# Both projections of the inputs ahead of both of the gates in the first mixer's units, and an input gate written in place

## The chip, the cores and the metric

The kernel runs on one core of a Trainium2 chip. The metric is the device time of one execution in microseconds; lower is better. The five engines of the core work side by side, each through its own row of instructions: TensorE (PE; its weight loads are listed apart as PEld), VectorE (DVE), ScalarE (ACT), GpSimd (POOL) and SyncE (SP), which starts the transfers.

## What is computed

One layer of a decoder: 2048 tokens of 1024 channels in f32. After a norm one projection feeds two mixers. The first is a gated linear recurrence over time behind a short convolution, with 512 channels in eight blocks; the second has four heads with a state of 128 x 128 each. Their outputs are joined, projected back and added; then a gate with a small embedding follows, and a last norm. The reference, cut to what matters:

```python
def rg_lru(x, wa, ba, wx, bx, lam):                     # first mixer
    xb = x.reshape(B, T, 8, 64)
    r = sigmoid(einsum('btgi,gij->btgj', xb, wa).reshape(B, T, 512) + ba)   # recurrence gate
    i = sigmoid(einsum('btgi,gij->btgj', xb, wx).reshape(B, T, 512) + bx)   # input gate
    log_a = -8.0 * r * softplus(-lam)
    a = exp(log_a)
    mult = sqrt(-expm1(2.0 * log_a))                    # 1 at the first token
    u = mult * (i * x)
    h[t] = a[t] * h[t - 1] + u[t]                       # written as an associative scan
    return h

def hgrn2_branch(q, fz, iv, g, lb, norm_w):             # second mixer
    f = lb + (1.0 - lb) * sigmoid(fz)
    k = (1.0 - lb) * sigmoid(-fz)
    o = gla_chunked(silu(q) * 128 ** -0.5, k, log(f), iv)   # scores, state per chunk, outputs
    return rms_norm_heads(o, norm_w) * silu(g)

u = rms_norm(x)
xa, ga, qb, fb, ib, gb = split(u @ w_in)
xa = causal_depthwise_conv(xa, conv_w, conv_b)          # width 4
ya = rg_lru(xa, ...) * silu(ga)
yb = hgrn2_branch(qb, fb, ib, gb, ...)
h = x + concat([ya, yb]) @ w_out
h = h + sigmoid(rms_norm(h) @ w_gate + b_gate) * (p @ w_ple)
return rms_norm(h)
```

## The kernel before

**Tiling.** The tokens are taken in two halves of 1024, each half as two blocks of 512 (b = 0, 1; `NB` is 512, `HT` 1024). Channels lie on the 128 partitions. Every large product is made of three matmuls, since each f32 operand is split into a high and a low part: high by high, high by low and low by high (`mm3`, L87 to 89). A projection of 1024 input channels into 128 output channels for one block is thus 24 matmuls of 128x128 by 512 columns (`project`).

**Units.** In each half a list, `orders`, gives the order of the units: in the first half v, v, a 0, fq 0, g 0, a 1, fq 1, a 2, fq 2, a 3, fq 3, g 1; in the second a 3 stands at the end, behind g 1. A unit has 256 columns of the input weights. They are loaded in four pieces (`load_w`): SyncE starts the transfer, ScalarE copies the high part (`whi`, L76), GpSimd subtracts for the low part (`wlo`, L77). There are two buffers for a unit's weights and two for raw pieces, so the pieces for a later unit follow when an earlier unit's last matmul frees its buffer.

**A unit a** (`unit_a`) is one of four pairs of channel blocks of the first mixer. For each block of tokens it projects the inputs xa; ScalarE brings them out of PSUM (L409), VectorE makes the convolution (L411, L414: one product, and three products with a sum), and the result is split (`xp`, L420 and 421). Then it projects the gate path ga (sigmoid L324 on ScalarE, product L325 on VectorE). The gates r and i are small matmuls on the split inputs, each followed by two sigmoids of 64 partitions (`gates`, L381): the matmul of c = 0 leaves r of the lower 64 channels in the lower partitions of its result and the input gate of the other 64 channels in the upper ones; c = 1 is the other way round. Here the input gate of every 64 channels goes into a tile `is_` in the partitions in which the result has it, and two copies on VectorE (L389) bring each part to its channels' partitions in `i_`. Behind block 1's gates stands the recurrence over all 1024 tokens (`recur`): the product of i and the inputs (L391), tanh, exponential, square and root on ScalarE (L392 to 396), two products (L395, L399), the scan (L400), the product with ga (L402) and the store of y.

**A unit fq** (`unit_b`, called for each of the two blocks) is one head of the second mixer: f and kn by sigmoids (L436, 437), f scaled (L438), a running product cp (scan, L443), its reciprocal rc (L445), factors per chunk (mid, rmid, dec), q (L465 to 467), kn (L460), then scores (L475, four matmuls of 128 columns from q and kn, masked into `sc_buf` at L477), a transposed kn (L481), the state's updates (L489 to 498, through `sp`, L497) and the outputs.

**Order.** Work that would wait is put off by a counter: `after(n, fn)` files a function and `tick()`, behind each projection, runs what is due. Gates are filed for three ticks later, scores for two. This gives the order in which the code hands out work; the order on each engine is then set by the framework's scheduler from its own estimates. Behind the units come the output projection, the gate and the last norm, in 16 tiles of 128 tokens; y goes through memory, and its split is L76 and L77 once more (`yh`, `yl`).

Of the kernel before, what the change touches and what calls it, by code (L numbers as in the profile page):

```python
# [8 lines left out]
F32 = mybir.dt.float32  # L9
# [10 lines left out]
P = 128  # L20
# [3 lines left out]
NB = 512  # L24
# [13 lines left out]
def hymba_block(ctx: ExitStack, tc: tile.TileContext, x, xT, pT, w_in, vecs, rg_w, w_out, w_gate,  # L38
# [191 lines left out]
    def tick():  # L230
        clock[0] += 1
        run_due()
# [82 lines left out]
    def half(hf):  # L315
        def project(w, half, b, name):
            acc = pj(name)
            cs = slice(half * P, (half + 1) * P)
            for k in range(KT):
                mm3(acc, w[0][:, k, cs], w[1][:, k, cs], u_hi[hf][b][:, k, :], u_lo[hf][b][:, k, :], k == 0, k == KT - 1)  # L320
            return acc

        def silu_into(dst, acc):
            nc.scalar.activation(dst, acc, AF.Sigmoid)  # L324
            nc.vector.tensor_tensor(dst, acc, dst, ALU.mult)  # L325
# [38 lines left out]
        def unit_a(w, j):  # L364
# [3 lines left out]
            ga = ap.tile([P, HT], F32, tag="ga", name=f"ga_{nm}")  # L368
            r = ap.tile([P, HT], F32, tag="r", name=f"r_{nm}")
            i_ = ap.tile([P, HT], F32, tag="i", name=f"i_{nm}")  # L370
            is_ = ap.tile([P, HT], F32, tag="th", name=f"is_{nm}")
            nc.vector.tensor_copy(xa[:, 0:3], halo[:, j, :])

            def gates(b, xp):
                s = slice(b * NB, (b + 1) * NB)
                for c in range(2):
                    pg = gl(f"rg_{nm}_{b}_{c}")
                    nc.tensor.matmul(pg, lhsT=g_hi[:, 2 * j + c, :], rhs=xp[c], start=True, stop=False)
                    nc.tensor.matmul(pg, lhsT=g_lo[:, 2 * j + c, :], rhs=xp[c], start=False, stop=True)
                    for dst, vb, h in ((r, V_BA, lohi[c]), (is_, V_BX, lohi[1 - c])):  # L380
                        nc.scalar.activation(dst[h, s], pg[h], AF.Sigmoid, bias=vec[h, vb + j:vb + j + 1])  # L381
                if b == 1:
                    recur()

            def recur():

                nc.vector.tensor_copy(halo[:, j, :], xa[:, HT:HT + 3])
                for c in range(2):
                    nc.vector.tensor_copy(i_[lohi[c]], is_[lohi[1 - c]])  # L389
                th = ap.tile([P, HT], F32, tag="th", name=f"th_{nm}")  # L390
                nc.vector.tensor_tensor(i_, i_, xc, ALU.mult)  # L391
                nc.scalar.activation(th, r, AF.Tanh, scale=sp8[:, j:j + 1])  # L392
# [13 lines left out]
            for b in range(2):  # L406
# [14 lines left out]
                    nc.vector.tensor_tensor(xp[c][o], xc[m, s], xp[c][m].bitcast(F32), ALU.subtract)  # L421
                after(3, lambda b=b, xp=xp: gates(b, xp))
                tick()
                acc = project(w, 1, b, f"ga_{nm}_{b}")
                silu_into(ga[:, s], acc)
                tick()

        def unit_b(w, j, b):
# [316 lines left out]
```

## Time and profile before

| | us |
|---|---|
| median of three runs | 1080.12 (1077.13 to 1081.25) |
| the profiled execution | 1079.53 |
| its span in the trace | 1077.3 |
| TensorE busy | 1035.1 (96%) |
| VectorE busy | 743.0 (69%) |
| ScalarE busy | 459.3 (43%) |
| GpSimd busy | 268.6 (25%) |

Busy times are sums over the span. The chain (part 4 of the profile) follows the work that ended last back from its end and gives the share of each engine in it. The mean granted clock of TensorE in this execution is 0.983 of full speed.

### The profile page before, as it was taken

The page shows a single profiled execution, that of the slowest core. Times are in us where ns is not written, and L with a number is a line of the kernel's source. Part 1 is how long each engine was busy: PE and PEld are TensorE (multiplying, and loading weights), DVE is VectorE, ACT ScalarE, POOL GpSimd, SP SyncE. Part 2 cuts the span into 40 slices and gives each one's busy share as a digit, 9 for nine tenths or more (in the row PEclk, how much of TensorE's full clock was granted, in tenths as well). Part 3 has the DMA queues.
Part 4 walks back from the last instruction along what each step waited for, and adds up shares of the span by engine and source line. Part 5 has one row for each costly group of instructions (what it writes and reads, how often), then busy time and mean ns, then how long its engine had stood idle before and what let it go on. Part 6 is the DMA issues. An engine that isn't in the chain of part 4 may idle for free.

```text
span 1077.3 us, 13808 instructions
## 1 busy us (share of the span) xinstructions
PE 1035.1 (96%) x5192; PEld 880.3 (82%) x5192; DVE 743.0 (69%) x1373; ACT 459.3 (43%) x779; POOL 268.6 (25%) x238
## 2 busy tenths in 40 slices
PE   8999999999999999999899999899999999999997
PEld 7998788787878998788787888677888888888886
DVE  6836746868688506745869839899766677666764
ACT  5546426556566225634656327642222222223222
POOL 5131221222223032221222217541112221111110
PEclk9999999999999999999999999899999999999998
DMA  9421111111136211111111038351122222111101
GB/s 332 138 78 42 59 59 40 59 59 59 59 128 233 70 59 59 59 59 40 59 59 53 26 123 273 112 162 64 64 84 83 74 69 74 64 64 59 44 25 54
DMA packets 55266, 91.10 MB, mean 85 GB/s; under 512 B 4640, under 2 KB 25120, under 8 KB 55200
## 3 DMA queue, kind: packets, MB, share of 16 engines
q1 hardware_dynamic: 55200, 90.22, 25.2%
q8 instruction: 41, 0.67, 0.2%
q14 instruction: 25, 0.20, 0.1%
HBM read 73.43 MB, written 16.78 MB: 84 GB/s over the span
## 4 chain that ended last, share of the span: by engine, by line
PE 76%; DVE 14%; DMA 4%; issue 2%; ACT 2%; POOL 1%; SPq 0%; POOLq 0%; DVEq 0%; ACTq 0%
PE g L88 7%; PE g L89 6%; PE g L87 6%; PE o L89 4%; PE o L87 4%; PE o L88 4%; PE q L88 3%; PE q L87 3%; PE v L89 2%; PE v L88 2%; DVE rc L445 2%; PE q L89 2%; PE v L87 2%; PE f L89 2%; PE f L88 2%; PE f L87 2%
## 5 line engine op out<-in xcount | busy, mean ns | idle before, releaser
L77 POOL TENSOR_TENSOR wlo<-raw_w,whi 128x512 fp32r<-128x512 f32 x92 | 126.2, 1384 | 300.0 <-ACT whi L76 299.6
L208 DVE STREAM_TRANSPOSE u2T<-u 32x256 f32<-32x256 f32 x256 | 111.6, 436 | 3.8
L89 PE MATMUL o<-wo_hi,yl 128*128 128x512 f32 x256 | 100.6, 394 | 3.5 <-POOL yl L77 3.5
L76 ACT ACTIVATE whi<-raw_w 128x512 fp32r<-128x512 f32 x96 | 58.0, 627 | 104.0 <-DMA raw_w<-in_w_in 81.9
L87 PE MATMUL o<-wo_hi,yh 128*128 128x512 f32 x256 | 100.7, 393 | 0.4 <-ACT yh L76 0.4
L88 PE MATMUL o<-wo_lo,yh 128*128 128x512 f32 x256 | 100.5, 392 | 0.0
L88 PE MATMUL g<-wg_lo,u2uh 128*128 128x512 f32 x224 | 88.0, 393 | 2.7 <-DVE wg_lo L77 2.7
L87 PE MATMUL g<-wg_hi,u2uh 128*128 128x512 f32 x224 | 88.1, 393 | 1.0 <-ACT wg_hi L76 1.0
L89 PE MATMUL g<-wg_hi,u2ul 128*128 128x512 f32 x224 | 87.6, 392 | 0.0
L89 PE MATMUL v<-whi,ul 128*128 128x256 f32 x224 | 64.7, 290 | 3.4 <-DVE ul L77 3.3
L88 PE MATMUL v<-wlo,uh 128*128 128x256 f32 x224 | 64.4, 288 | 0.8 <-POOL wlo L77 0.7
L87 PE MATMUL v<-whi,uh 128*128 128x256 f32 x224 | 64.3, 288 | 0.0
L77 POOL TENSOR_TENSOR yl<-raw_y,yh 128x512 fp32r<-128x512 f32 x32 | 43.2, 1354 | 78.1 <-ACT yh L76 64.4
L89 PEld LDWEIGHTS o<-wo_hi,yl 128*128 128x128 f32 x256 | 48.7, 190 | 14.2 <-POOL yl L77 4.0
L87 PEld LDWEIGHTS o<-wo_hi,yh 128*128 128x128 f32 x256 | 48.6, 190 | 11.0 <-ACT yh L76 0.9
L88 PEld LDWEIGHTS o<-wo_lo,yh 128*128 128x128 f32 x256 | 48.6, 190 | 10.1
L411 DVE TENSOR_SCALAR xc<-xa,vec 128x512 f32<-128x512 f32 x16 | 11.4, 712 | 65.6 <-ACT xa L409 65.6
L183 POOL TENSOR_TENSOR rs_f<-ms_f,neg_half 128x1 f32<-128x1 f32 x16 | 8.8, 549 | 189.9 <-DVE ms_f L181 175.9
L76 ACT ACTIVATE yh<-raw_y 128x512 fp32r<-128x512 f32 x32 | 19.9, 629 | 83.9 <-issue 47.5
L652 ACT ACTIVATE gt<-gt 128x512 f32<-128x512 f32 (+1 forms) x33 | 20.2, 613 | 82.0 <-DVE gt L651 81.9
L445 DVE RECIPROCAL rc<-cp 128x512 f32<-128x512 f32 x16 | 53.6, 3349 | 0.3
L497 ACT ACTIVATE sp<-state,dec 128x128 f32<-128x128 f32 x60 | 24.0, 401 | 69.6 <-DVE state L498 50.1
(221 smaller groups left out, 2915.2 us busy)
## 6 DMA issues: line engine op xcount, KB each, us to landing
raw_w<-in_w_in SPq DMA_DIRECT2D x96, 256.0 KB, 3.0
xcm<-in_xT SPq DMA_DIRECT2D x18, 512.0 KB, 4.3
xt<-in_x SPq DMA_DIRECT2D x16, 512.0 KB, 5.4
raw_y<-y_dram SPq DMA_DIRECT2D x32, 256.0 KB, 2.8
h<-in_x SPq DMA_DIRECT2D x16, 512.0 KB, 3.6
out<-h SPq DMA_DIRECT2D x15, 512.0 KB, 2.6
y_dram<-ga SPq DMA_DIRECT2D x16, 256.0 KB, 2.5
y_dram<-yb SPq DMA_DIRECT2D x16, 256.0 KB, 2.2
```

Source lines behind the costliest of these rows:

```text
L76: nc.scalar.activation(hi, src, AF.Identity)
L77: lo_eng.tensor_tensor(lo, src, hi.bitcast(F32), ALU.subtract)
L87: nc.tensor.matmul(acc, lhsT=lh, rhs=rh, start=first, stop=False)
L88: nc.tensor.matmul(acc, lhsT=lh, rhs=rl, start=False, stop=False)
L89: nc.tensor.matmul(acc, lhsT=ll, rhs=rh, start=False, stop=last)
L183: nc.gpsimd.tensor_tensor(rs, ms, neg_half[:, 0:1], ALU.pow)
L208: nc.vector.transpose(dst[32 * j:32 * j + 32, :, 32 * i:32 * i + 32], src[32 * i:32 * i + 32, :, 32 * j:32 * j + 32])
L411: nc.vector.tensor_scalar(xc[:, s], xa[:, b * NB:b * NB + NB], cw[:, 0:1], vec[:, V_CONVB + j:V_CONVB + j + 1], ALU.mult, ALU.add)
L445: nc.vector.reciprocal(rc, cp)
L497: nc.scalar.activation(sp, state[j], AF.Identity, scale=dec[:, n])
L652: nc.scalar.activation(gt, gt, AF.Sigmoid)
```

## The change

In `unit_a` the loop over the blocks becomes two loops: xa of block 0 and xa of block 1 first, each with its convolution and its filing of the gates, and then ga of block 0 and ga of block 1. The number of ticks is the same, so the gates of block 1, filed at the second tick instead of the third, come due one tick earlier: at the end of the unit instead of behind the next unit's first projection. The recurrence goes with them. And the tile `is_` goes: ScalarE writes the input gate straight into the partitions of its channels in `i_`, from the partitions of the matmul's result on the other side, and the two copies of 64 partitions by 1024 fall away.

```diff
--- before.py
+++ after.py
@@ -368,7 +368,6 @@
             ga = ap.tile([P, HT], F32, tag="ga", name=f"ga_{nm}")
             r = ap.tile([P, HT], F32, tag="r", name=f"r_{nm}")
             i_ = ap.tile([P, HT], F32, tag="i", name=f"i_{nm}")
-            is_ = ap.tile([P, HT], F32, tag="th", name=f"is_{nm}")
             nc.vector.tensor_copy(xa[:, 0:3], halo[:, j, :])
 
             def gates(b, xp):
@@ -377,16 +376,15 @@
                     pg = gl(f"rg_{nm}_{b}_{c}")
                     nc.tensor.matmul(pg, lhsT=g_hi[:, 2 * j + c, :], rhs=xp[c], start=True, stop=False)
                     nc.tensor.matmul(pg, lhsT=g_lo[:, 2 * j + c, :], rhs=xp[c], start=False, stop=True)
-                    for dst, vb, h in ((r, V_BA, lohi[c]), (is_, V_BX, lohi[1 - c])):
-                        nc.scalar.activation(dst[h, s], pg[h], AF.Sigmoid, bias=vec[h, vb + j:vb + j + 1])
+
+                    for dst, vb, h in ((r, V_BA, lohi[c]), (i_, V_BX, lohi[1 - c])):
+                        nc.scalar.activation(dst[lohi[c], s], pg[h], AF.Sigmoid, bias=vec[h, vb + j:vb + j + 1])
                 if b == 1:
                     recur()
 
             def recur():
 
                 nc.vector.tensor_copy(halo[:, j, :], xa[:, HT:HT + 3])
-                for c in range(2):
-                    nc.vector.tensor_copy(i_[lohi[c]], is_[lohi[1 - c]])
                 th = ap.tile([P, HT], F32, tag="th", name=f"th_{nm}")
                 nc.vector.tensor_tensor(i_, i_, xc, ALU.mult)
                 nc.scalar.activation(th, r, AF.Tanh, scale=sp8[:, j:j + 1])
@@ -421,8 +419,9 @@
                     nc.vector.tensor_tensor(xp[c][o], xc[m, s], xp[c][m].bitcast(F32), ALU.subtract)
                 after(3, lambda b=b, xp=xp: gates(b, xp))
                 tick()
+            for b in range(2):
                 acc = project(w, 1, b, f"ga_{nm}_{b}")
-                silu_into(ga[:, s], acc)
+                silu_into(ga[:, b * NB:(b + 1) * NB], acc)
                 tick()
 
         def unit_b(w, j, b):
```

VectorE in the first half, from the kn of unit fq 1's block 0 to the mask of its scores. A name ends in unit, block and a number; `th`, `i`, `r` and `ga` belong to the recurrence of unit a 1, which runs just ahead of fq 1. Before:

```order
L460 SCALAR_TENSOR_TENSOR kn_1_0_1681<-kn_1_0_1681,omlb,rc_1_0_1689 128x512
L395 SCALAR_TENSOR_TENSOR th_1_1714<-xc_1_1495,th_1_1714 128x1024
L438 TENSOR_SCALAR f_1_1_1782<-f_1_1_1782,omlb,lb 128x512
L440 COPY d_115<-f_1_1_1782 128x8
L441 MEMSET f_1_1_1782 128x8
L443 SCALAR_TENSOR_TENSOR cp_1_1_1789<-f_1_1_1782,d_115 128x512
L398 MEMSET th_1_1714 128x1
L399 TENSOR_TENSOR i_1_1498<-i_1_1498,th_1_1714 128x1024
L445 RECIPROCAL rc_1_1_1791<-cp_1_1_1789 128x512
L450 COPY mid_1_1_1793<-cp_1_1_1789 128x4
L400 SCALAR_TENSOR_TENSOR r_1_1497<-r_1_1497,h_last,i_1_1498 128x1024
L477 COPY_PREDICATED sc_buf_113<-keep,sc_1_0_1804 128x512
```

Now, from the recurrence's scan to the same unit's q of block 1:

```order
L398 SCALAR_TENSOR_TENSOR r_1_1494<-r_1_1494,h_last,i_1_1495 128x1024
L466 TENSOR_TENSOR q_1_0_1747<-q_1_0_1747,cp_1_0_1708 128x512
L459 SCALAR_TENSOR_TENSOR kn_1_0_1702<-kn_1_0_1702,omlb,rc_1_0_1710 128x512
L437 TENSOR_SCALAR f_1_1_1776<-f_1_1_1776,omlb,lb 128x512
L399 COPY h_last<-r_1_1494 128x1
L400 TENSOR_TENSOR ga_1_1493<-ga_1_1493,r_1_1494 128x1024
L439 COPY d_115<-f_1_1_1776 128x8
L440 MEMSET f_1_1_1776 128x8
L442 SCALAR_TENSOR_TENSOR cp_1_1_1783<-f_1_1_1776,d_115 128x512
L444 RECIPROCAL rc_1_1_1785<-cp_1_1_1783 128x512
L449 COPY mid_1_1_1787<-cp_1_1_1783 128x4
L465 SCALAR_TENSOR_TENSOR q_1_1_1836<-q_1_1_1811,q_1_1_1836 128x512
```

The recurrence's scan and its product with ga stood behind the reciprocal of block 1; now the scan stands ahead of the kn of block 0 and the product right behind f of block 1.

ScalarE in the same unit, from the first pieces of the next unit a's weights (`whi_8`) to q of block 0, before:

```order
L76 ACTIVATE whi_8_1861<-raw_w_8_0_1863 128x512
L76 ACTIVATE whi_8_1861<-raw_w_8_1_1867 128x512
L324 ACTIVATE ga_1_1496<-ga_1_1_1610 128x512
L76 ACTIVATE whi_8_1861<-raw_w_8_2_1871 128x512
L76 ACTIVATE whi_8_1861<-raw_w_8_3_1875 128x512
L436 ACTIVATE f_1_0_1680<-f_1_0_1655 128x512
L437 ACTIVATE kn_1_0_1681<-f_1_0_1655 128x512
L381 ACTIVATE r_1_1497<-rg_1_1_0_1701,vec 64x512
L381 ACTIVATE is_1_1499<-rg_1_1_0_1701,vec 64x512
L381 ACTIVATE r_1_1497<-rg_1_1_1_1706,vec 64x512
L381 ACTIVATE is_1_1499<-rg_1_1_1_1706,vec 64x512
L465 ACTIVATE q_1_0_1753<-q_1_0_1728 128x512
```

Now, from the gate path's last sigmoid to f:

```order
L324 ACTIVATE ga_1_1493<-ga_1_1_1606 128x512
L381 ACTIVATE r_1_1494<-rg_1_1_0_1633,vec 64x512
L381 ACTIVATE i_1_1495<-rg_1_1_0_1633,vec 64x512
L381 ACTIVATE r_1_1494<-rg_1_1_1_1638,vec 64x512
L381 ACTIVATE i_1_1495<-rg_1_1_1_1638,vec 64x512
L390 ACTIVATE th_1_1644<-r_1_1494,sp_127 128x1024
L76 ACTIVATE whi_8_1855<-raw_w_8_2_1865 128x512
L391 ACT_TABLE_LOAD
L391 ACTIVATE r_1_1494<-r_1_1494,nsp_128 128x1024
L76 ACTIVATE whi_8_1855<-raw_w_8_3_1869 128x512
L435 ACT_TABLE_LOAD
L435 ACTIVATE f_1_0_1701<-f_1_0_1676 128x512
```

f and kn of block 0 stood ahead of the gates of block 1; now the four gate sigmoids, the tanh, the exponential and two loads of function tables stand ahead of f.

TensorE at the scores of block 0 of the same unit, before, inside the projection of q of block 1:

```order
L88 MATMUL q_1_1_1817<-ul_1_389,whi_5_1637 128x512
L89 MATMUL q_1_1_1817<-uh_1_388,wlo_5_1638 128x512
L87 MATMUL q_1_1_1817<-uh_1_388,whi_5_1637 128x512
L475 MATMUL sc_1_0_1804<-q_1_0_1753,kn_1_0_1681 128x128 x4
L481 MATMUL kT_1_0_1810<-ident,kn_1_0_1681 128x128 x4
L88 MATMUL q_1_1_1817<-ul_1_389,whi_5_1637 128x512
L89 MATMUL q_1_1_1817<-uh_1_388,wlo_5_1638 128x512
L87 MATMUL q_1_1_1817<-uh_1_388,whi_5_1637 128x512
```

Now, inside the next unit's first projection:

```order
L87 MATMUL q_1_1_1811<-uh_1_388,whi_5_1658 128x512
L88 MATMUL q_1_1_1811<-ul_1_389,whi_5_1658 128x512
L89 MATMUL q_1_1_1811<-uh_1_388,wlo_5_1659 128x512
L87 MATMUL xa_2_0_1879<-uh_0_210,whi_8_1855 128x512
L88 MATMUL xa_2_0_1879<-ul_0_211,whi_8_1855 128x512
L89 MATMUL xa_2_0_1879<-uh_0_210,wlo_8_1856 128x512
L87 MATMUL xa_2_0_1879<-uh_0_210,whi_8_1855 128x512
L88 MATMUL xa_2_0_1879<-ul_0_211,whi_8_1855 128x512
L89 MATMUL xa_2_0_1879<-uh_0_210,wlo_8_1856 128x512
L474 MATMUL sc_1_0_1798<-q_1_0_1747,kn_1_0_1702 128x128 x4
L480 MATMUL kT_1_0_1804<-ident,kn_1_0_1702 128x128 x4
```

The scores moved eleven matmuls back, out of q and into xa of unit a 2. The scores of block 1 (`sc_1_1`) stand 70 matmuls of projections behind the end of f of block 1 in the order before, and 60 in the new one.

## Rows read from the trace of the kernel before

**Rows 1.** Page, parts 1 and 4: busy us; shares of the last chain

```profile
PE 1035.1 (96%) x5192; PEld 880.3 (82%) x5192; DVE 743.0 (69%) x1373; ACT 459.3 (43%) x779; POOL 268.6 (25%) x238
...
PE 76%; DVE 14%; DMA 4%; issue 2%; ACT 2%; POOL 1%; SPq 0%; POOLq 0%; DVEq 0%; ACTq 0%
```

**Rows 2.** List of waits: who for whom, total us, times, longest

```profile
PE sc L475 <- DVE kn L460: 16.1, 7, 3.0
...
PE o L89 <- POOL yl L77: 3.5, 1, 3.5
```

**Rows 3.** TensorE by time, 188 to 207: start, us, instruction [idle before]

```profile
189.84 1.05 PE L475 MATMUL sc<-q,kn 128*128 128x128 f32 x8
...
202.08 0.39 PE L87 MATMUL ga<-uh,whi 128*128 128x512 f32 x1
...
203.44 0.39 PE L87 MATMUL ga<-uh,whi 128*128 128x512 f32 x1
206.20 1.02 PE L475 MATMUL sc<-q,kn 128*128 128x128 f32 x7 [2.37 <-DVE kn L460]
```

**Rows 4.** ScalarE by time, 168 to 190

```profile
169.34 0.58 ACT L324 ACTIVATE ga<-ga 128x512 f32<-128x512 f32 x1
173.22 0.63 ACT L76 ACTIVATE whi<-raw_w 128x512 fp32r<-128x512 f32 x1 [3.31 <-DMA raw_w<-in_w_in]
...
174.80 0.58 ACT L436 ACTIVATE f<-f 128x512 f32<-128x512 f32 x1
...
175.75 0.67 ACT L381 ACTIVATE r<-rg,vec 64x512 f32<-64x512 f32 x1
...
177.71 0.68 ACT L381 ACTIVATE is<-rg,vec 64x512 f32<-64x512 f32 x1
...
183.31 1.15 ACT L392 ACTIVATE th<-r,sp 128x1024 f32<-128x1024 f32 x1 [2.42 <-DVE i L389]
184.48 1.28 ACT L393 ACT_TABLE_LOAD   x1
185.77 1.15 ACT L393 ACTIVATE r<-r,nsp 128x1024 f32<-128x1024 f32 x1
```

**Rows 5.** VectorE by time, 168 to 210

```profile
175.41 1.35 DVE L438 TENSOR_SCALAR f<-f,omlb,lb 128x512 f32<-128x512 f32 x1 [4.77 <-ACT f L436]
...
178.41 0.69 DVE L389 COPY i<-is 64x1024 f32<-64x1024 f32 x1
...
184.05 1.22 DVE L391 TENSOR_TENSOR i<-i,xc 128x1024 f32<-128x1024 f32 x1
...
188.05 1.23 DVE L395 SCALAR_TENSOR_TENSOR th<-xc,th 128x1024 f32<-128x1024 f32 x1 [0.84 <-ACT xc L394]
189.96 0.55 DVE L438 TENSOR_SCALAR f<-f,omlb,lb 128x512 f32<-128x512 f32 x1 [0.69 <-ACT f L436]
...
192.85 0.06 DVE L398 MEMSET th<- 128x1 f32 x1 [0.73 <-ACT th L396]
...
199.62 0.73 DVE L477 COPY_PREDICATED sc_buf<-keep,sc 128x512 f32<-128x512 uint32 x1
...
200.81 1.26 DVE L455 TENSOR_TENSOR dec<-cp,mid 128x3 f32<-128x3 f32 x1
...
205.31 0.74 DVE L460 SCALAR_TENSOR_TENSOR kn<-kn,omlb,rc 128x512 f32<-128x512 f32 x1
```

**Rows 6.** GpSimd by time, 168 to 202

```profile
173.94 2.55 POOL L77 TENSOR_TENSOR wlo<-raw_w,whi 128x512 fp32r<-128x512 f32 x2 [2.40 <-ACT whi L76]
193.87 2.70 POOL L77 TENSOR_TENSOR wlo<-raw_w,whi 128x512 fp32r<-128x512 f32 x2 [17.38 <-ACT whi L76]
198.97 3.08 POOL L77 TENSOR_TENSOR wlo<-raw_w,whi 128x512 fp32r<-128x512 f32 x2 [2.40 <-ACT whi L76]
```

**Rows 7.** VectorE by time, 412 to 455, one row

```profile
448.12 1.92 DVE L402 TENSOR_TENSOR ga<-ga,r 128x1024 f32<-128x1024 f32 x1
```

**Rows 8.** A stretch: us, busy PE PEld DVE ACT POOL, PEclk, DMA, GB/s

```profile
207.60:211.00 3.40, 3.40 (x18) 3.30 (x17) 2.67 (x6) 2.51 (x5) 0.00 (x0) 0.51 0.10 34
```

## The prediction

> **What bounds the kernel now.** I read the page first, then the list of who waited for whom, then one stretch in order of time, engine by engine. TensorE is busy 96% of the span and holds three quarters of the chain that ended last; the next holder is VectorE with 14% [rows 1]. So an edit can gain only where TensorE stands still, and the list of waits says where that is: 16.1 us in seven waits of one kind, the scores of a head of the second group (line 475) waiting for kn from VectorE (line 460) [rows 2]. The only other long wait that this change can touch is one of 3.5 us for yl at the start of the output projection [rows 2].
>
> The seven waits stand behind units of the first group: unit a hands its recurrence to VectorE and ScalarE just as the next unit fq needs both. I take one of them as the model, the scores of block 1 of fq 1 in the first half. TensorE's last matmul ahead of it starts at 203.44 and the scores at 206.20, of which 2.37 us is the wait [rows 3]; TensorE was ready at 203.83. From 202.08 to 203.44 are six matmuls of 512 columns [rows 3], so one costs 0.227 us.
>
> **What the change takes away.** Two copies of 0.69 us leave VectorE in each of the eight units a (the 178.41 row is one, [rows 5]): 1.4 us a unit, 11 us in all, but only what lies on the chain to kn counts. The product of the input gate and the input (184.05, 1.22 us, of which some 0.1 overlaps the next) now stands ahead of f, where VectorE is idle, so 1.1 us leave the chain too. VectorE also stood idle three times in the chain, 0.84, 0.69 and 0.73 us, each time for ScalarE [rows 5]; in the new order other work stands in each of these places. And f of block 0, held at 175.41 for 0.8 us beyond the 0.55 of its twin at 189.96, no longer meets GpSimd's work. From the start of f at 175.41 to the end of the last kn at 206.05 are 30.6 us [rows 5]; without these pieces, 30.6 - 1.4 - 1.1 - 2.3 - 0.8 = 25.0 us.
>
> **What it adds: f comes later.** In the kernel before, ScalarE evicts f right behind the weights' last piece, at 174.80 [rows 4]. Now both gates, the tanh, a table load, the exponential and a second table load stand ahead of it. By the rows: the gate path's sigmoid ends at 169.92; four gate sigmoids take 2.64 us (175.75 to 178.39); the tanh 1.15, which gives 173.7; a weight piece 0.63 (its data are there at 173.22); table load 1.28; exponential 1.15; weight piece 0.63; table load 1.28; f itself 0.58 [rows 4]. The sum is 179.2, against 175.4: f is 3.8 us later. Nothing covers that, since VectorE has nothing else to do between 174 and 179: the rest of the recurrence needs the exponential, which comes as late. The chain then ends at 179.2 + 25.0 = 204.2, 1.9 us earlier than the 206.05 of before.
>
> On the table load a rule speaks against the change: the Trainium skill, "ScalarE: Activation LUTs", section "What ACT_TABLE_LOAD costs", gives about 2.66 us for a switch, of which 1.38 us are a drain. The rows have 1.28 us for the load, the exponential 0.01 us behind it and the load 0.02 us behind the tanh [rows 4]: the trace shows no drain. By the Trainium skill's price the total below would be some 19 us longer, an estimate of 1106 us.
>
> **What it moves: TensorE's turn.** Counted from the end of f 1, before, 19 matmuls of q stood ahead of the scores of block 0, and 5 + 17 + 7 + 22 more ahead of those of block 1, 70 in all; now 30 and 30 do. TensorE reaches block 1's scores ten matmuls sooner, at 203.83 - 10 x 0.227 = 201.6. With kn at 204.2 and 0.15 us from its end to the first scores [rows 3, 5] the wait is 2.7 us, against 2.4. So what VectorE gains is given back by TensorE's arriving earlier: 0.3 us lost. Counted alike, five stretches have nine or ten matmuls fewer and two have six; those two gain 0.6 us each by the same sum.
>
> **What else stands in the new place.** GpSimd works in pairs of about 1.3 us on weight pieces. The pair at 193.87 fell beside VectorE's reciprocal and held nobody up; the pair at 173.94 fell on f, which took 1.35 us; the second piece of the pair at 198.97 fell on dec, which took 1.26 us for 3 columns [rows 5, 6]. In the new order the earlier of the two later pairs follows the last matmul of q 1, whose weights' buffer it fills: that matmul ends about 191.1 (189.84 and five matmuls, [rows 3]), ScalarE's copy of 0.63 follows, and GpSimd starts about 191.9. From f of block 1 to its kn are 16.1 us (189.96 to 206.05); from f of block 0 to its kn the new order has th where that stretch has ga, 1.2 us each, and lacks the idle 0.73, dec's hold of 1.1 and the masking of scores with the short operations beside it (199.62 to 200.81), some 1.3: 12.9 are left [rows 5]. So VectorE reaches f of block 1 at 179.2 + 12.9 = 192.1, and right behind it stands the product ga, which took 1.92 us where it met such a pair [rows 7], 0.7 more than the product of the same shape at 184.05. So between 0 and 0.8 + 0.7, with an op of a few columns between them that can lose 0.5 more, is added. Both pieces of the pair are still to run when f arrives, so I take a value nearer to the upper end, 1.1 us. The hold on dec stays as it was.
>
> Per stretch that is 0.3 + 1.1 = 1.4 us more on five, and 1.1 - 0.6 = 0.5 us more on two: 8.0 us. In the first stretch of each half the gate sigmoids of block 0 now queue behind two more splits, each of about the 0.63 us of a weight piece; half of that hidden, 0.6 us each. Together 9 us.
>
> **Edits with one answer.** The input gate's sigmoid, 0.68 us beside its twin's 0.67 [rows 4], now writes to the other 64 partitions; the twin is the nearest row, so I take it as nothing. Were it twice as long, f would come 1.4 us later per stretch; were it shorter, it could save at most as much. The store of y moves ahead of two weight loads on SyncE and waits for ga; queued behind it are those loads, then ScalarE's copies and GpSimd's later pair. They come about 1 us later for weights used some 30 us later, so TensorE does not see it. The scores of block 0 come eleven matmuls behind their 189.84 [rows 3], at 192.3, when kn of block 0 has just ended at 192.1: 0 to 0.5 us. The state updates now stand between the convolutions of the next unit a, and the outputs of block 0 may wait 0 to 0.5 us for them in four stretches; 1 us in all for both. At the output projection GpSimd does the same pieces ahead of yl in another order and the recurrence ends earlier: the 3.5 us [rows 2] may go wholly or grow by one piece of 1.3; I take 2 us gained.
>
> The clock: behind the model's wait the granted clock is 0.51 for 3.4 us [rows 8], the 1.2 GHz level, after TensorE had stood for 2.37 us. At half speed that loses up to 1.7 us. I take as many such dips as before and put 5 us either way into the range.
>
> **The sum** goes against the profiled execution, 1079.5 us with its span of 1077.3, 0.6 under the median of 1080.1: 1079.5 + 9 + 1 - 2 = 1087.5; I say 1087.
>
> **Rivals.** First, GpSimd's pair misses f and ga: 1079.5 + 9 - 7 x 1.1 + 1 - 2 = 1080, no change. My two starts, 191.9 and 192.1, are close, which speaks for it; that two pieces follow each other speaks against. The Trainium skill ("SBUF — State Buffer", section "Who interferes with whom") says that whichever of the two engines starts first holds the shared ports for its whole instruction; by that, f starting just ahead would be saved and ga still held, which lies between this sum and the forecast.
>
> Second, the other side: kn ahead of TensorE. It decides in the model stretch from 2.7 us: if f comes that much sooner than summed, the seven waits vanish and the time is 1079.5 - 16.1 - 2 = 1061; half of it gives 1070. Fewer copies and an earlier product speak for it; against it, f cannot pass the two table loads.
>
> Third, the stretch ahead of the second half: there the norm of the next rows stands in VectorE's queue between f and kn, and needs a load that starts only when the recurrence frees its buffer. A miss adds the length of such a load, some 5 us: 1092.
>
> Fourth, a table load costs twice what the row says, in the new place between two users: 2 x 1.28 x 7 = 18 us more, 1105. The rows speak against it.
>
> **How the numbers follow.** Forecast 0.45, first rival 0.27, second 0.13 (most of it half-way), third 0.12, fourth 0.03. A measurement of this kernel tells about 0.5% from no change, here 1074.7 to 1085.5. The forecast's own range is 1081 to 1096, and a quarter of it lies under 1085.5. Faster: 0.14. Same: 0.25 of the first rival and 0.11 of the forecast, 0.36. Slower: 0.50. Leaving out a tenth at either end, the range is 1073 to 1098.
>
> **What would show it.** Right: f of block 0 evicted 3.5 to 4 us later, counted from the gate path's last matmul; the scores still waiting for kn seven times, 18 to 28 us in total; f or ga of block 1 held beside GpSimd. Wrong: those waits under 10 us in all, f in its old place on ScalarE, or a long new wait of TensorE, above all for sp (line 497 before) or for the norm ahead of the second half.

## The result and the profile after

The changed kernel takes 1087.24 us in the median (1086.9 to 1088.89, five runs); the kernel before has 1080.12 us (1077.13 to 1081.25, five runs). The ratio is 1.0073, with a 95% interval of 1.0054 to 1.0091: slower by 0.7%. The profiled execution's span is 1084.7 us, 7.4 more than before.

The page of the changed kernel, parts 1 and 4, with the columns of [rows 1]:

```profile
PE 1036.5 (96%) x5192; PEld 880.3 (81%) x5192; DVE 732.6 (68%) x1357; ACT 459.9 (42%) x779; POOL 277.0 (26%) x238
...
PE 62%; DVE 20%; ACT 8%; issue 5%; DMA 3%; POOL 1%; SPq 0%; POOLq 0%; DVEq 0%; ACTq 0%
```

VectorE has 16 instructions less, the two copies of the eight units a, and 10.4 us less of busy time. GpSimd has the same 238 instructions and is busy 8.4 us longer. ScalarE, with 2% of the chain in [rows 1], now holds 8% of it: the chain runs through the gates, the tanh, the exponential and f.

The list of waits of the changed kernel (who waited for whom: us in total, times, longest), to be read beside [rows 2]:

```profile
PE sc L474 <- DVE kn L459: 16.8, 8, 4.4
PE sc L474 <- DVE d L439: 6.8, 3, 3.1
...
PE o L87 <- DVE h L619: 3.0, 1, 3.0
...
PE o L89 <- POOL yl L77: 2.1, 1, 2.1
PE o L87 <- ACT yh L76: 1.7, 1, 1.7
```

The first two lines are one kind of wait, the scores for kn; where block 1's copy d stands right behind that kn on VectorE, the profile names d as what ended it. Together they are 23.6 us in eleven stops, against 16.1 in seven. The whole idle time of TensorE grew from 34.2 to 39.8 us: 7.6 more at the scores, 2.8 less in four waits around the turn of the halves and behind it, 0.8 more at the start, and nothing at the output, where two waits in front of the first tile (1.7 and 2.1 us) stand for the one of 3.5 in [rows 2] and its neighbour, and the 3.0 us for h take the place of most of the waits for the gate's weights (3.7 before, 0.9 now). TensorE's busy time is 1.4 us longer with the same 5192 matmuls, and 0.5 us more lie behind its last one.

### The profile page after: what moved, and what is told of

It is laid out like the page before. It is cut to its first block, busy times and chain, and to the rows that moved or that the text cites. A ratio compares the mean times of both kernels' runs of the same rounds, so it can differ in the third digit from the quotient of the medians.

```text
span 1084.7 us, 13781 instructions
## 1 busy us (share of the span) xinstructions
PE 1036.5 (96%) x5192; PEld 880.3 (81%) x5192; DVE 732.6 (68%) x1357; ACT 459.9 (42%) x779; POOL 277.0 (26%) x238
## 4 chain that ended last, share of the span: by engine, by line
PE 62%; DVE 20%; ACT 8%; issue 5%; DMA 3%; POOL 1%; SPq 0%; POOLq 0%; DVEq 0%; ACTq 0%
PE g L89 7%; PE g L88 7%; PE g L87 7%; PE o L87 4%; PE o L88 4%; PE o L89 4%; DVE rc L444 4%; PE v L89 2%; PE ga L87 2%; PE v L87 2%; PE ga L88 2%; PE v L88 2%; PE ga L89 2%; DMA raw_w<-in_w_in 2%; DVE r L398 1%
## 5 line engine op out<-in xcount | busy, mean ns | idle before, releaser
L77 POOL TENSOR_TENSOR yl<-raw_y,yh 128x512 fp32r<-128x512 f32 x32 | 46.7, 1463 | 70.2 <-ACT yh L76 70.2
L87 PEld LDWEIGHTS o<-wo_hi,yh 128*128 128x128 f32 x256 | 48.7, 190 | 15.7 <-DVE h L619 3.5
L444 DVE RECIPROCAL rc<-cp 128x512 f32<-128x512 f32 x16 | 53.6, 3349 | 0.3
L516 POOL TENSOR_TENSOR rs<-ms,neg_half 128x4 f32<-128x4 f32 x16 | 18.4, 1152 | 135.9 <-DVE ms L514 135.9
L87 PE MATMUL g<-uh,whi 128*128 128x512 f32 x128 | 52.5, 410 | 0.0
```

The lines of the kernel that those rows point to most:

```text
L77: lo_eng.tensor_tensor(lo, src, hi.bitcast(F32), ALU.subtract)
L87: nc.tensor.matmul(acc, lhsT=lh, rhs=rh, start=first, stop=False)
L444: nc.vector.reciprocal(rc, cp)
L516: nc.gpsimd.tensor_tensor(rs[:, :, 0], ms, neg_half, ALU.pow)
```

## The model stretch, forecast and trace

The stretch of [rows 3 to 6] is at 170 to 208 us in the changed kernel; its gate path's last matmul ends at 170.82 (168.42 before), by the first of these rows for the kernel before and the second for the changed one:

```profile
168.03 0.39 PE L89 MATMUL ga<-uh,wlo 128*128 128x512 f32 x1
170.42 0.40 PE L89 MATMUL ga<-uh,wlo 128*128 128x512 f32 x1
```

ScalarE there, in order of time (start, us, instruction, idle before it):

```profile
171.72 0.58 ACT L324 ACTIVATE ga<-ga 128x512 f32<-128x512 f32 x1
...
175.01 1.16 ACT L390 ACTIVATE th<-r,sp 128x1024 f32<-128x1024 f32 x1
...
176.70 1.28 ACT L391 ACT_TABLE_LOAD   x1
178.00 1.15 ACT L391 ACTIVATE r<-r,nsp 128x1024 f32<-128x1024 f32 x1
...
179.69 1.28 ACT L435 ACT_TABLE_LOAD   x1
180.98 0.60 ACT L435 ACTIVATE f<-f 128x512 f32<-128x512 f32 x1
```

f starts 10.16 us behind the gate path's last matmul, against 6.38 before: 3.8 us later, as summed. VectorE and GpSimd in the same stretch:

```profile
181.62 0.55 DVE L437 TENSOR_SCALAR f<-f,omlb,lb 128x512 f32<-128x512 f32 x1 [5.37 <-ACT f L435]
...
194.21 1.51 DVE L437 TENSOR_SCALAR f<-f,omlb,lb 128x512 f32<-128x512 f32 x1
...
195.70 2.23 DVE L400 TENSOR_TENSOR ga<-ga,r 128x1024 f32<-128x1024 f32 x1
...
204.38 1.23 DVE L454 TENSOR_TENSOR dec<-cp,mid 128x3 f32<-128x3 f32 x1
...
206.87 0.74 DVE L459 SCALAR_TENSOR_TENSOR kn<-kn,omlb,rc 128x512 f32<-128x512 f32 x1
```

```profile
194.09 2.77 POOL L77 TENSOR_TENSOR wlo<-raw_w,whi 128x512 fp32r<-128x512 f32 x2 [13.06 <-ACT whi L76]
203.09 2.51 POOL L77 TENSOR_TENSOR wlo<-raw_w,whi 128x512 fp32r<-128x512 f32 x2 [6.23 <-ACT whi L76]
```

GpSimd's pair starts 0.12 us ahead of f and holds it and the product ga: 1.51 instead of 0.55, 2.23 instead of 1.21. dec is held as before. And TensorE at the end of the stretch:

```profile
207.75 1.62 PE L474 MATMUL sc<-q,kn 128*128 128x128 f32 x6 [3.81 <-DVE kn L459]
```

From f to the last kn are 26.0 us where 30.6 stood, f is 3.8 us later, and TensorE stands 3.81 us instead of the 2.37 of [rows 3].

## The experiments

Each was made from the kernel before or the changed kernel by the diff shown. Medians of one kernel differ by a few us between groups of runs (the kernel before has 1080.12, 1078.63, 1076.94 and 1079.63), so ratios to the runs of before beside them are given.

**The write in place alone.** From the kernel before:

```diff
-            is_ = ap.tile([P, HT], F32, tag="th", name=f"is_{nm}")
-                    for dst, vb, h in ((r, V_BA, lohi[c]), (is_, V_BX, lohi[1 - c])):
-                        nc.scalar.activation(dst[h, s], pg[h], AF.Sigmoid, ...
+                    for dst, vb, h in ((r, V_BA, lohi[c]), (i_, V_BX, lohi[1 - c])):
+                        nc.scalar.activation(dst[lohi[c], s], pg[h], AF.Sigmoid, ...
-                for c in range(2):
-                    nc.vector.tensor_copy(i_[lohi[c]], is_[lohi[1 - c]])
```

> Only the input gate written in place; the projections keep the order of the kernel before. Theory (the new order of the projections, which puts the recurrence ahead of f on ScalarE, is what costs; the write in place alone gains): f of block 0 stays about 6.4 us behind the gate path's last matmul, the copies' 1.4 us leave VectorE's chain and the tanh no longer waits 2.4 us for them, TensorE comes 0.7 us (first half) or 1.4 us (second half) sooner at the scores; the waits for kn shrink from 16.1 to under 5 us and the time is about 1066 us, 1062 to 1072. Rival (the sigmoid written across partitions costs as much as the copies, or the copies were hidden): 1078 to 1083 us.

Measured: 1081.91 us (1079.58 to 1091.88), ratio 1.0043 (1.0016 to 1.0069). Slower by 0.4%, and my theory missed by 16 us. The profiled execution was a long one, 1091.88 us, so its rows serve for the order and the holds, not for the sum. f of block 0 did keep its place (6.3 us), but the chain from it to the last kn still takes 30.4 us in the model stretch. ScalarE and VectorE there:

```profile
185.81 0.60 ACT L462 ACTIVATE q<-q 128x512 f32<-128x512 f32 x1
...
187.38 1.28 ACT L393 ACT_TABLE_LOAD   x1
189.57 1.06 ACT L393 ACTIVATE th<-th 128x1024 f32<-128x1024 f32 x1 [0.91 <-DVE th L392]
190.65 1.28 ACT L433 ACT_TABLE_LOAD   x1
191.95 0.60 ACT L433 ACTIVATE f<-f 128x512 f32<-128x512 f32 x1
```

```profile
177.72 1.48 DVE L435 TENSOR_SCALAR f<-f,omlb,lb 128x512 f32<-128x512 f32 x1 [4.67 <-ACT f L433]
...
192.58 0.55 DVE L435 TENSOR_SCALAR f<-f,omlb,lb 128x512 f32<-128x512 f32 x1 [0.56 <-ACT f L433]
...
195.49 2.36 DVE L399 TENSOR_TENSOR ga<-ga,r 128x1024 f32<-128x1024 f32 x1
...
197.91 2.17 DVE L440 TENSOR_TENSOR_SCAN cp<-f,d 128x512 f32<-128x512 f32 x1
...
207.39 0.73 DVE L457 SCALAR_TENSOR_TENSOR kn<-kn,omlb,rc 128x512 f32<-128x512 f32 x1
```

GpSimd beside it:

```profile
195.46 3.53 POOL L77 TENSOR_TENSOR wlo<-raw_w,whi 128x512 fp32r<-128x512 f32 x2 [16.55 <-ACT whi L76]
```

With the copies gone, ScalarE takes the tanh and the exponential ahead of q and f of block 1 behind the root, so that four table loads stand between the two f where two stood; VectorE waits for f. Then the scan and the product ga stand ahead of the running product of block 1, in the place where GpSimd's pair falls: ga and that running product cp are held by 1.1 and 0.9 us, and two small operations by 0.6 each. With f of block 0 the holds in this chain are 4.2 us, against 2.3 in the kernel before: most of what the copies gave went there.

**The order alone.** From the changed kernel, the tile and the copies put back:

```diff
+            is_ = ap.tile([P, HT], F32, tag="th", name=f"is_{nm}")
-                    for dst, vb, h in ((r, V_BA, lohi[c]), (i_, V_BX, lohi[1 - c])):
-                        nc.scalar.activation(dst[lohi[c], s], pg[h], AF.Sigmoid, ...
+                    for dst, vb, h in ((r, V_BA, lohi[c]), (is_, V_BX, lohi[1 - c])):
+                        nc.scalar.activation(dst[h, s], pg[h], AF.Sigmoid, ...
+                for c in range(2):
+                    nc.vector.tensor_copy(i_[lohi[c]], is_[lohi[1 - c]])
```

> Only the order of the projections changed; the input gate goes through its own tile and two copies as before. Theory: the copies stand between the gate sigmoids and the tanh, whose buffer they free, so f comes 0.8 to 1.4 us later than in the changed kernel in each of seven stretches: 1087 + 7 x 1.1 = 1095 us, 1092 to 1098. Rival (the copies fall into VectorE's idle time and cost nothing; the write in place is worth nothing here): 1086 to 1089 us.

Measured: 1084.23 us (1082.27 to 1088.32), ratio 1.0050 (1.0031 to 1.0068). The rival is nearer, though the time lies 2 us under its range: the copies put f 0.6 us later in the model stretch (10.79 us behind the gate path's last matmul), but cost nothing in the total. Each half of the change is slower by itself, 0.4% and 0.5%, and the two together 0.7%; whether they add, these intervals do not tell.

**The gates put back.** From the changed kernel:

```diff
-                after(3, lambda b=b, xp=xp: gates(b, xp))
+                after(3 + b, lambda b=b, xp=xp: gates(b, xp))
```

> The changed kernel with the gates of block 1 filed for four ticks later instead of three, so that they and the recurrence stand behind the next unit's first projection again, as in the kernel before. Theory (the early recurrence is the cost, not the projections' order itself): f is back at about 6.4 us behind the gate path's last matmul, and the time is that of the write in place alone, about 1066 us, 1062 to 1072. Rival (projecting both xa first costs by itself, by VectorE's convolutions and TensorE's earlier turn): within 4 us of the changed kernel's 1087.

Measured: 1085.62 us (1084.62 to 1087.18), ratio 1.0059 (1.0037 to 1.0081). f of block 0 is back at 6.3 us in the model stretch, and the time is not: my theory missed by 20 us, and the rival's number came, though the run does not show its reason. ScalarE and VectorE run as in the write in place alone: f of block 1 waits for the root and two table loads, ga takes 2.34 and cp 2.17 us, and the chain has 30.2 us. So "f comes later" is a true term of the sum, but taking it back in this way does not give the time back: the chain's length goes with it.

**No low parts.** Both kernels without the low parts that GpSimd makes of the weights (all units but v). From either:

```diff
-        lo = wst.tile([P, KT, 256], F32R, tag="wlo", name=f"wlo_{hf}_{n}", bufs=2)
+        lo = hi if n in NOLO else wst.tile([P, KT, 256], F32R, tag="wlo", name=f"wlo_{hf}_{n}", bufs=2)
...
-        split(hi, lo, raw, lo_eng)
+        if hi_only:
+            nc.scalar.activation(hi, raw, AF.Identity)
+        else:
+            split(hi, lo, raw, lo_eng)
```

On the changed kernel:

> The changed kernel without GpSimd's low parts of the weights, except those of the units v: the matmuls read the high parts in their place, so their number and the order on VectorE up to the second wait stay. Theory (VectorE's operations beside GpSimd's pieces are held about 1.0 us each, and those holds are on the chain to kn): q and kn of block 0 in the first wait, f, ga and dec in the second, f in the third, rc and ga in the fifth, f in the sixth, some 9 us in all: 1078 us, 1074 to 1082, and no VectorE operation of the chain is stretched. Rival (the holds are covered by ScalarE's lateness): 1085 to 1088.

Measured: 1059.91 us (1058.19 to 1062.54), ratio 0.9825 (0.9791 to 0.9858): three times the gain that I had listed. The waits for kn fall by 19.0 us, to 4.6, and TensorE's busy time by 8.7. On the kernel before:

> The kernel before, with the same left out as in the run without low parts: GpSimd makes no low parts of the weights but those of the units v, and the matmuls read the high parts. Theory A (the change gives VectorE's gain back only where GpSimd holds it; without the pieces the two orders are about level): the holds of some 1.9 us per wait (f of block 0, dec) leave the chain, the seven waits fall from 16.1 to about 4 us and TensorE stands fewer times at the low clock: 1062 us, 1057 to 1068, against 1060 of the changed kernel without them. Rival B (the change costs by itself, by f's coming later and TensorE's earlier turn, whatever GpSimd does): 7 us under the changed kernel without low parts, 1053.

Measured: 1063.22 us (1061.68 to 1064.36), ratio 0.9864 (0.9833 to 0.9895). Theory A is the nearer: without the pieces the changed kernel is no longer the slower one, but 3.3 us the faster (0.4% by the ratios, whose intervals overlap); with them it is 7.1 us the slower. The waits for kn are 4.6 us in the changed kernel without them and 3.7 in the kernel before without them. Busy times of the changed kernel and of the kernel before without low parts (part 1 of the page):

```profile
PE 1027.8 (97%) x5192; PEld 872.3 (82%) x5192; DVE 707.9 (67%) x1357; ACT 459.4 (43%) x779; POOL 163.5 (15%) x158
```

```profile
PE 1028.6 (97%) x5192; PEld 873.5 (82%) x5192; DVE 723.6 (68%) x1373; ACT 461.1 (43%) x779; POOL 166.4 (16%) x158
```

The counts of VectorE's instructions are those of the full kernels, so the differences of its busy time are holds: 743.0 - 723.6 = 19.4 us before, 732.6 - 707.9 = 24.7 us after. The change took 15.7 us of work from VectorE (723.6 - 707.9) and put 5.3 us of holds in. And in the model stretch of the changed kernel without low parts nothing is held; from f (175.30) to the end of the last kn are 22.6 us:

```profile
175.30 0.55 DVE L441 TENSOR_SCALAR f<-f,omlb,lb 128x512 f32<-128x512 f32 x1 [5.54 <-ACT f L439]
...
187.90 0.54 DVE L441 TENSOR_SCALAR f<-f,omlb,lb 128x512 f32<-128x512 f32 x1
...
188.42 1.21 DVE L404 TENSOR_TENSOR ga<-ga,r 128x1024 f32<-128x1024 f32 x1
...
195.79 0.15 DVE L458 TENSOR_TENSOR dec<-cp,mid 128x3 f32<-128x3 f32 x1
...
197.20 0.75 DVE L463 SCALAR_TENSOR_TENSOR kn<-kn,omlb,rc 128x512 f32<-128x512 f32 x1
```

22.6 against 26.0 are 3.4 us of holds in this stretch: f 0.96, ga 1.02, dec 1.08, and rmid 0.3.

**No table loads.** From the changed kernel:

```diff
-                nc.scalar.activation(th, r, AF.Tanh, scale=sp8[:, j:j + 1])
-                nc.scalar.activation(r, r, AF.Exp, scale=nsp8[:, j:j + 1])
+                nc.scalar.activation(th, r, AF.Sigmoid, scale=sp8[:, j:j + 1])
+                nc.scalar.activation(r, r, AF.Sigmoid, scale=nsp8[:, j:j + 1])
...
-                nc.scalar.activation(th, th, AF.Sqrt)
+                nc.scalar.activation(th, th, AF.Sigmoid)
```

> The changed kernel with sigmoids in place of tanh, exponential and root in the recurrence, so that ScalarE loads no function table between the units (the values are not the reference's). Theory (f is late by the work ahead of it on ScalarE, and of its lateness the two table loads of 1.28 us are 2.56 us): f of block 0 comes 2.6 us sooner in each of seven stretches and the waits of 23.6 us fall by as much where they are that long: 1071 us, 1067 to 1077. Rival (GpSimd's holds move with it and keep the last kn where it is, as in the two runs that put f back): 1083 to 1089. If a load costs 2.66 us, as the Trainium skill, 'ScalarE: Activation LUTs', section 'What ACT_TABLE_LOAD costs', has it, f comes 5.3 us sooner.

Measured: 1065.11 us (1062.26 to 1066.69), ratio 0.9879 (0.9850 to 0.9908). ScalarE in the model stretch, whose gate path's last matmul ends at 172.12:

```profile
176.32 1.15 ACT L390 ACTIVATE th<-r,sp 128x1024 f32<-128x1024 f32 x1
...
177.90 1.14 ACT L391 ACTIVATE r<-r,nsp 128x1024 f32<-128x1024 f32 x1
...
179.46 0.57 ACT L435 ACTIVATE f<-f 128x512 f32<-128x512 f32 x1
```

f comes 7.34 us behind it instead of 10.16, 2.8 sooner: the two loads' 2.56, and 0.1 us each by which two neighbours now overlap. By the higher price that the prediction weighs, it would have been 5.3. So f's lateness does cost, as the prediction has it. But the run takes away 31 of the kernel's 33 loads, two behind f in each stretch too (kn comes 3.5 us sooner in the model stretch, not 2.8), and the kernel before without its loads was not run. The time fell by 22 us, 4 more than 7 x 2.56 and 2 past the end of my range; f of block 0 is held by 0.6 us in five of the seven stretches, where it now meets a piece of GpSimd's.

**The low parts on VectorE.** Here nothing is left out: the low parts of all units but v are made by VectorE instead of GpSimd.

```diff
-            load_split(hi[:, s], lo[:, s], w_in[n][:, s], nc.vector if raw_pool and q % 2 else nc.gpsimd,
+            load_split(hi[:, s], lo[:, s], w_in[n][:, s], nc.vector if (raw_pool and q % 2) or (UNITS[n][0] != "v") else nc.gpsimd,
```

On the changed kernel, on the write in place alone, and on the kernel before:

> The changed kernel with all low parts of the weights but those of the units v made on VectorE instead of GpSimd; nothing is left out. Theory (GpSimd's holds, 3.2 us of the chain from f to the last kn, cost more than the work itself): three pieces of about 0.65 us come into the chain, no operation is held, and TensorE's scores stand 13 matmuls later in most stretches; the waits fall under 5 us: 1064 us, 1058 to 1072. Rival (VectorE's queue is the bound, and 56 us more work there lengthen it): 1085 or more.

> The input gate written in place in the old order of the projections, with the low parts of the weights (but those of the units v) on VectorE. If the holds were what kept the write in place alone from gaining, 1066 us, 1060 to 1074; if ScalarE's two table loads ahead of f of block 1 keep the chain at 30 us, within 5 us of the 1082 of the write in place alone.

> The kernel before with the low parts of the weights (but those of the units v) on VectorE and nothing else changed. Theory: GpSimd's holds were most of the loss, and the write in place is worth little once TensorE's scores stand 81 matmuls behind f of block 1 (73 in the kernel with the write in place, 70 before): 1062 us, 1058 to 1066. Rival (the copies' 1.4 us in each of seven chains come back as waits): 1059.4 + 7 x 1.4 = 1069 us.

Measured: 1067.44 us, ratio 0.9905 (0.9881 to 0.9929), on the changed kernel; 1059.42 us, 0.9824 (0.9795 to 0.9853), with the write in place alone; 1059.94 us, 0.9830 (0.9788 to 0.9871), on the kernel before. The same subtraction takes 0.65 us on VectorE (two in 1.29) where it took 1.3 on GpSimd, and nothing around it is held in the model stretch of any of the three. The second time is 0.6 us under its expected range, the other two lie in theirs. VectorE in the model stretch of the second:

```profile
188.90 1.21 DVE L399 TENSOR_TENSOR ga<-ga,r 128x1024 f32<-128x1024 f32 x1
...
190.17 1.23 DVE L440 TENSOR_TENSOR_SCAN cp<-f,d 128x512 f32<-128x512 f32 x1
...
195.18 1.29 DVE L77 TENSOR_TENSOR wlo<-raw_w,whi 128x512 fp32r<-128x512 f32 x2
...
198.93 0.74 DVE L457 SCALAR_TENSOR_TENSOR kn<-kn,omlb,rc 128x512 f32<-128x512 f32 x1
199.59 1.32 DVE L77 TENSOR_TENSOR wlo<-raw_w,whi 128x512 fp32r<-128x512 f32 x2
```

ga and the scan cp, 2.36 and 2.17 us in the write in place alone, are back at 1.21 and 1.23, and the second pair of pieces stands behind kn. The table loads stand where they stood and the chain still has 28.4 us, but TensorE no longer waits. Beside the kernel before with the same pieces moved, the write in place is worth nothing measurable, 0.5 us.

The new order, though, costs 8.0 us beside the write in place alone and 7.5 us beside the kernel before, as much as with the pieces on GpSimd (7.1), and here only one of VectorE's operations in these stretches is held, by 1.0 us in the fourth (by a piece of a unit v). The waits for kn are 5.1 us, against 0.5 and 1.6; TensorE's busy time is 2.9 and 3.9 us longer. The rest was not taken apart.

Nor is the gain of the kernel before, 1.7%, shown to come from the holds. VectorE's busy time grew by 28.6 us (771.6 against 743.0), and the chain from f to the last kn has 30.9 us in the model stretch where it had 30.6. TensorE's order changed with it: block 1's scores stand 81 matmuls behind f of block 1 where 70 stood, 11 x 0.227 = 2.5 us, as much as the wait had been. The scores of that stretch, whose kn ends at 201.97:

```profile
202.52 0.72 PE L475 MATMUL sc<-q,kn 128*128 128x128 f32 x5
```

Two variants of the second, in the set of units whose low parts VectorE makes:

```diff
-nc.vector if (raw_pool and q % 2) or (UNITS[n][0] != "v") else nc.gpsimd,
+nc.vector if (raw_pool and q % 2) or (hf == 1 or UNITS[n][0] != "v") else nc.gpsimd,
```

> The write in place in the old order with the low parts on VectorE, those of the second half's units v too. If holds in the stretch between the halves are what keeps 3 us of small waits there (rs, o, v between 316 and 341 us), 1057 us; if VectorE is full there, 1059 to 1062.

```diff
-nc.vector if (raw_pool and q % 2) or (UNITS[n][0] != "v") else nc.gpsimd,
+nc.vector if (raw_pool and q % 2) or (UNITS[n] in (("fq", 1), ("fq", 2), ("fq", 3), ("a", 1))) else nc.gpsimd,
```

> The write in place in the old order, with only those low parts on VectorE that fall behind f of block 1 (the weights of fq 1, 2 and 3 and of a 1); GpSimd keeps the others, so f of block 0 is held by 0.6 to 0.9 us again and TensorE's scores stand 74 or 71 matmuls behind f of block 1. Theory (the pieces behind f of block 1 do most of the harm): 1062 us, 1058 to 1068. Rival (every piece counts alike, ten of some twenty units' pieces moved): half way between 1082 and 1059, 1070 us.

Measured: 1057.52 us, ratio 0.9804 (0.9769 to 0.9839), for the first, the lowest time here and 2.0% under the kernel before; its interval overlaps that of the run without the change, so between its two expectations little is decided. The second has 1061.39 us, 0.9839 (0.9805 to 0.9874): eight units' pieces moved give nearly all of what moving all gives, as the theory has it. In its model stretch kn comes 1.5 us sooner than in the write in place alone, and TensorE's scores stand 74 matmuls behind f of block 1 instead of 67, 1.4 us later; the run does not part the two.

## Where the prediction was right, and where not

The time forecast was 1087, the time measured 1087.24, and the range held it. It is not all merit: several terms were off and cancelled.

*f later on ScalarE*: summed 3.8 us, measured 3.8 in the model stretch and 3.5 to 5.0 in five others. *The chain from f to the last kn*: summed 25.0 plus 1.1 of holds, measured 26.0. *The wait there*: summed 2.7 plus 1.1, measured 3.81. *The waits for kn in all*: 18 to 28 us were to show it right, 23.6 came, but in eleven stops, not seven. *The sigmoid's write across partitions*: taken as nothing; it takes 0.68 us as before.

**The hold of f and ga** is the term that was mis-sized: 1.1 us, between 0 and 1.5 (and 0.5 for a small one), and 2.0 came in the model stretch. I had bounded f's loss by 0.8, from a row where it met a pair late, and ga's by 0.7; both were held by about 1.0. The sum came out all the same because the rest of the chain was 1.0 us shorter than summed (26.0 - 2.0 against 25.0), 0.3 of it between the two f: 12.6 us from one to the other instead of 12.9 (13.0 by its own terms).

**The scores of block 0** were taken at 0 to 0.5 us. Half of all the waiting is there. The seven waits of before, at block 1's scores, and what stands in their places now (us, in the order of the stretches):

| stretch | before, block 1 | after, block 0 | after, block 1 |
|---|---|---|---|
| 1, behind a 0 of the first half | 2.40 | 4.44 | 0.00 |
| 2, the model | 2.37 | 0.00 | 3.81 |
| 3 | 1.98 | 1.73 | 0.58 |
| 4 | 1.41 | 0.09 | 3.58 |
| 5, behind a 0 of the second half | 2.68 | 3.14 | 0.96 |
| 6 | 3.03 | 1.92 | 0.81 |
| 7 | 2.20 | 0.43 | 2.24 |
| sum | 16.1 | 11.8 | 12.0 |

By stretch, the sum had 2.0, 1.4, 1.4, 0.5, 2.0, 1.4 and 0.5 us more of waiting, and 2.0, 1.4, 0.3, 2.3, 1.4, -0.3 and 0.5 came: three as summed, the others off both ways, 9.2 against 7.6 in all. That the total came so near is in part luck.

The model stood for one order of VectorE only. In stretches 3, 5, 6 and 7 the scheduler put the product ga and f of block 1 ahead of the kn of block 0. VectorE in the fifth, and TensorE's scores of block 0:

```profile
442.08 1.45 DVE L457 TENSOR_TENSOR rc<-rc,mid 128x256 f32<-128x256 f32 x1
...
443.52 2.25 DVE L400 TENSOR_TENSOR ga<-ga,r 128x1024 f32<-128x1024 f32 x1
...
446.75 0.74 DVE L459 SCALAR_TENSOR_TENSOR kn<-kn,omlb,rc 128x512 f32<-128x512 f32 x1
```

```profile
447.63 0.57 PE L474 MATMUL sc<-q,kn 128*128 128x128 f32 x3 [3.14 <-DVE d L439]
```

kn of block 0 waits for ga, which GpSimd holds by 1.0, and for rc, held by 1.0 as well. What TensorE stood at block 0's scores it does not stand again at block 1's, so the total came out.

**The first stretch** was given 0.6 us more. f came 6.6 us later there, not 3.8 + 0.6: the convolution of block 1 ends late on VectorE, ScalarE takes the gate path's first sigmoid behind it and a table load, and the gate path's last one only 3.8 us behind its matmul. There GpSimd's pair also fell on block 0's q and kn:

```profile
110.09 2.35 DVE L398 TENSOR_TENSOR_SCAN r<-r,h_last,i 128x1024 f32<-128x1024 f32 x1
112.36 1.69 DVE L466 TENSOR_TENSOR q<-q,cp 128x512 f32<-128x512 f32 x1
113.97 1.75 DVE L459 SCALAR_TENSOR_TENSOR kn<-kn,omlb,rc 128x512 f32<-128x512 f32 x1
```

```profile
110.63 4.54 POOL L77 TENSOR_TENSOR wlo<-raw_w,whi 128x512 fp32r<-128x512 f32 x2 [10.19 <-ACT whi L76]
```

**The output projection** was to gain 2 us and gained nothing. **The turn of the halves**, for which the third rival had a loss of 5 us, gave 2.8 us back instead: the norm waited 1.6 us for kT in the kernel before and not at all now. **The clock** was to have as many dips as before: within the span TensorE was granted half speed for 38.4 us against 36.8, well within the 5 us either way.

**The rivals.** The first, that GpSimd's pair misses f and ga, did not happen here; but without any pieces the two kernels are level to 3 us. The second, kn ahead of TensorE, is nearly what the low parts on VectorE bring about: in the changed kernel the waits for kn fall to 5.1 us and the time, 1067.44, lies between the rival's 1061 and its half-way 1070. The fourth, dear table loads, is shown wrong by the run without them.

**How far the cause is shown.** I put the loss down first to f's coming later and TensorE's coming sooner, with GpSimd's hold as a further term. In the model stretch, counted in us from the end of the gate path's last matmul, TensorE could take up block 1's scores (their start less the wait) and kn was ready at:

| kernel | TensorE | end of kn | wait |
|---|---|---|---|
| before | 35.41 | 37.63 | 2.37 |
| changed | 33.13 | 36.79 | 3.81 |
| before, no low parts | 35.25 | 34.42 | 0 |
| changed, no low parts | 33.36 | 33.80 | 0.58 |
| before, low parts on VectorE | 37.75 | 37.20 | 0 |
| changed, low parts on VectorE | 36.07 | 35.92 | 0 |

In the first pair TensorE is 2.3 us sooner and kn 0.8, as the prediction sums it (2.3, and 1.9 less 1.1 of holds). Without the pieces it is much the same, 1.9 and 0.6. So in this stretch the step from the old order to the new one does not come from GpSimd. What GpSimd's pieces do is to make kn late in both kernels, by 3 us here; without them the kernel before has 0.8 us in hand, which covers most of the step. The 10.4 us between losing 7.1 and gaining 3.3 show that the loss needs a kn that is late, not that GpSimd's holds alone are its cause: with the pieces on VectorE next to nothing is held, and the new order loses 7.5 us again, though not in the model stretch.

Putting f back, in two runs, gained at most 0.3% against the changed kernel's own order, by ratios whose intervals overlap: the chain then lengthens by ScalarE's loads ahead of f of block 1 and by other holds. What the other six stretches lose was followed for the first and the fifth only.

## What to carry over

A chain made shorter gains nothing if the engine that waits for it comes sooner by more: here kn came 0.8 us earlier and TensorE 2.3. Before an operation is taken from VectorE, look also at what GpSimd runs beside the place where the next one will land: work removed from a chain moves the rest of it, and here f and ga of block 1 moved into GpSimd's pieces. A subtraction of 1.3 us on GpSimd held an operation of VectorE by up to about 1.0, and done on VectorE it took 0.65 us; but where moving it pays, as in the kernel before, see whether the chain became shorter or the scheduler placed the waiting work later. And a stretch taken as a model stands for the others only if the order on the waited-for engine is the same in them; it is worth a look at each.

## What the runs showed of the hardware

VectorE and GpSimd hold each other in both directions. GpSimd's pair of pieces took 4.54 us instead of 2.55 where VectorE's scan of 2.35 us had started 0.54 us ahead of it; then VectorE's q and kn, 0.68 and 0.74 us elsewhere, took 1.69 and 1.75. A product of 3 columns took 1.23 us instead of 0.15. The reciprocal, 3.35 us, was not lengthened in any of these kernels (3349 ns in the mean before and after, 3357 at most), though pairs ran beside it. That agrees with the Trainium skill, "SBUF — State Buffer", section "Who interferes with whom", which says that whoever starts first keeps the shared ports for its whole instruction, and that an operation of VectorE with one input from SBUF is left alone outside of its modes with two ports; a tensor_scalar such as f is among those that it says can enter such a mode.

A table load costs its 1.28 us and no more beside its neighbours here: two of them taken away brought f 2.8 us sooner. The Trainium skill, "ScalarE: Activation LUTs", section "What ACT_TABLE_LOAD costs", has 2.66 us for each; this measurement decides against it for this kernel.

Behind the second longest of TensorE's stops, 3.81 us at the model stretch's scores, the granted clock was at its lower level of 1.2 GHz for longer than behind the 2.37 us of the kernel before [rows 8]; the columns are those of [rows 8]:

```profile
207.75:212.00 4.25, 4.25 (x20) 4.25 (x21) 4.18 (x9) 2.15 (x5) 0.00 (x0) 0.50 0.01 4
212.00:216.00 4.00, 4.00 (x19) 3.43 (x19) 1.10 (x3) 1.19 (x3) 0.00 (x0) 0.82 0.00 0
```

In the three kernels with the low parts on VectorE (all units but v) it was there for 23 to 25 us of the span, against 36.8 before, and TensorE's busy time is 3.4 to 7.3 us shorter with the same matmuls. That part of what shorter waits give comes by the clock fits these figures; no run parts it from the rest.
